# mLSTM of a hybrid block: the products of queries with states of both directions in three fp32r passes, the decay applied behind the product, and decay rows loaded one head ahead and masked in place

## The chip, the cores and the metric

One core of one Trainium2 chip runs the whole kernel as one program. The metric is device time in microseconds of one execution, the median of several runs. The engines named below are PE (TensorE matmul) with its weight loads (PEld), DVE (VectorE), ACT (ScalarE), POOL (GpSimd) and SP (SyncE, which only issues DMAs here).

## The reference, cut to what matters

The layer is one encoder block on 512 tokens of 1024 channels, all in float32: a combined projection, three token mixers (a bidirectional mLSTM with four heads of 128, neighbourhood attention, cross-attention into 256 memory tokens), a gated merge, an output projection, a gated FFN with a convolution, and a final norm. The change lies in the mLSTM. For one direction and one head the reference computes, chunk by chunk:

```python
inter_log = a + m_prev[..., None]
m_j = jnp.maximum(inter_log, jnp.max(D, axis=-1))
qk = jnp.einsum('bhcjd,bhcsd->bhcjs', q, k)
P = jnp.exp(D - m_j[..., None]) * qk
inter_w = jnp.exp(inter_log - m_j)
num = jnp.einsum('bhcjs,bhcsd->bhcjd', P, v) + inter_w[..., None] * jnp.einsum('bhcde,bhcje->bhcjd', C_prev, q)
den = jnp.sum(P, axis=-1) + inter_w * jnp.einsum('bhce,bhcje->bhcj', n_prev, q)
h = num / jnp.maximum(jnp.abs(den), jnp.exp(-m_j))[..., None]
```

The first term of `num` comes from keys inside the chunk; the second is the query times the state `C_prev` of all earlier chunks (for the backward direction, later ones), weighted by a decay per query. `den` is the same with the normaliser `n_prev`. The outputs of both directions are added and normalised per token and head.

## The kernel before, in words

**The big products.** A float32 product is made of three fp32r passes: each operand is split into a high part, rounded to fp32r, and the low rest; `mm3` (L212 to L215) issues high x high, high x low and low x high into one PSUM bank. The weights come in blocks of 128x1024 (512 KB) on SP's DMA queue into three raw buffers (L159). ACT makes the high part (L195), DVE the low part (L196), each in two halves per block, into four buffers for each part. All projections work on `mm` PSUM banks (four), the attention work on `at` banks (four). A helper `split_act` (L217 to L220) splits an activation in the same way.

**The order of the work.** The mixers are Python generators. `proj` emits one projection of 24 passes, and `step` (L1022) lets the oldest generator run for some of its steps in between: 1.25 steps after a projection of 512 columns in this stage (`RB`), 0.7 after a memory projection of 256 (`RM`). A scheduler then places the instructions on each engine, mostly in the order emitted, and later where an operand is not ready yet. PE, DVE and ACT each run their own list strictly in order. Small pieces of DVE and ACT work can be put off through the list `late`, which is emptied by `flush` in the second pass group of the next projection, or at the start of `states`.

**The mLSTM.** The 512 tokens are four blocks J of 128 and not the reference's chunks of 64: the same function in larger pieces. `ml_prep` (L549) makes the gates' cumulative sums; the rows cu - m, one number a token for each direction and head, go to DRAM as `rd`. `spread` (L621) makes the columns per block: `bi` (key side), `mh` (the maximum carried into the block), `wt` (weights of the keys in a state), `dec` (decay from state to state). Then, for each head h:

- `load_R` (L651): SP loads `rd[d, h]`, spread over all 128 partitions, into a tile R of 128x512, one for each direction; `mask` (L660) adds the triangle mask into a second tile `rm`. R and rm share four buffers, so one head fills them.
- `keys` (L666): four transposes of the keys, the split of the inner blocks' keys, and in `weigh` the values with weights, split as well.
- `states` (L696): the sums of each block into two `at` banks (blocks 1 and 2 with `mm3` on 258 columns for both directions, L709; blocks 0 and 3 as plain fp32 products of 129 columns, L707), then DVE and ACT chain them into three states a direction, `C[d][i]`, 128x129 each (128 values and the normaliser).
- `weights_J` (L726): the score product of keys and queries (L730, plain fp32, into columns 384 to 511 of a new `at` bank); ACT makes exp(rm + bi) for both directions (L734) and exp(R + mh) for each direction that has a state (L738); DVE multiplies the first with the scores (L739) and the second with the queries (L741).
- `values_J` (L744): on PE, for each direction, the weights times the values (L749) and, with `inter`, the weighted queries times the state (L751), both plain fp32 with 129 columns into columns 0 to 259 of the same bank. Then the denominators (ACT absolute value, DVE maximum and reciprocal), the sum of both directions in H (L757, L758) and the squares' sum (L760).
- `normalise` (L762): POOL raises to the power -0.5, DVE scales H (L769). `emit_y` (L771) transposes H and applies the output gate.

One step holds the weights of block J and the values of block J - 1, so the values of block 3 fall into the next head's first step, ahead of its states. `load_R` and `keys` of the next head are emitted in the step of block 3.

Of the kernel before, what the change touches and what calls it, by code (L numbers as in the profile page):

```python
# [17 lines left out]
P = 128  # L18
S = 512
# [91 lines left out]
def hybrid_block(ctx, tc, xg, xT, memT, wflat, vecs, gbias, nabias, outa, outb, outc):  # L111
# [437 lines left out]
    def ml_prep():  # L549
# [71 lines left out]
        def spread():  # L621
# [20 lines left out]
            ml.update(bi=bi, mh=mh, wt=wt, dec=dec)  # L642

# [3 lines left out]
    def ml_all():  # L647
# [3 lines left out]
        def load_R(h):  # L651
            R, rm = [], []
            for d in range(2):
                t = tp.tile([P, S], F32, tag="R", name=nm("R"), bufs=4)
                SY.dma_start(t, rd[d, h].partition_broadcast(P))
                R.append(t)
                rm.append(tp.tile([P, S], F32, tag="R", name=nm("R"), bufs=4))
            return R, rm

        def mask(R, rm):  # L660
            for d in range(2):
                with tc.issue_after(st["dve"]):
                    V.tensor_tensor(rm[d].rearrange("p (j c) -> p j c", j=4), R[d].rearrange("p (j c) -> p j c", j=4),
                                    msk[d].unsqueeze(1).to_broadcast([P, 4, P]), op=ALU.add)

        def keys(h):  # L666

# [5 lines left out]
            kh, kl = [u[:, o:o + 2 * P] for o in (1040, 1296)]  # L673
            ke = scr(2 * P)
            ew = tp.tile([P, S], F32, tag="H", name=nm("ew"), bufs=4)
            ew = [ew[:, o:o + 129] for o in (0, 132)]
# [3 lines left out]
            A.activation(ke.rearrange("p (j c) -> p j c", j=2), pt.rearrange("p (j c) -> p j c", j=4)[:, 0:4:3, :], AF.Copy)  # L680

# [11 lines left out]
            late.append(weigh)  # L693
            return (ke, kh, kl), (ew, wh, wl), C

        def states(h, k, w, C):  # L696

# [6 lines left out]
            for J in range(NT):  # L704
# [6 lines left out]
            for d in range(2):  # L711
                t = tp.tile([P, 2 * M], F32, tag="nab", name=nm("C"))
                C.append([t[:, o:o + 129] for o in (0, 132, 264)])
# [10 lines left out]
        def weights_J(h, J, R, rm):  # L724

            bi, mh = ml["bi"], ml["mh"]  # L726
# [3 lines left out]
            PE.matmul(kq, kT[:, hs], qT[:, hs], start=True, stop=True)  # L730
            E = tp.tile([P, 4, P], F32, tag="E", name=nm("E"))
            for d in range(2):
                with tc.issue_after(st["act"]):
                    A.activation(E[:, d, :], rm[d][:, js], AF.Exp, bias=bi[:, d, J, h:h + 1])  # L734
            ds = [d for d in range(2) if 0 <= J - 1 + 2 * d < NT]
            for d in ds:
                with tc.issue_after(st["act"]):
                    A.activation(E[:, 2 + d, :], R[d][:, js], AF.Exp, bias=mh[:, J - 1 + 2 * d, d, h:h + 1])  # L738
            V.tensor_tensor(E[:, 0:2, :], E[:, 0:2, :], kq.unsqueeze(1).to_broadcast([P, 2, P]), op=ALU.mult)  # L739
            a, b = 2 + ds[0], 3 + ds[-1]  # L740
            V.tensor_tensor(E[:, a:b, :], E[:, a:b, :], qT[:, hs].unsqueeze(1).to_broadcast([P, b - a, P]), op=ALU.mult)  # L741
            return E, ps

        def values_J(h, J, E, ps, C, H, ss):  # L744
            js = slice(J * P, (J + 1) * P)
            pv = ps[:, :260].rearrange("p (d c) -> p d c", d=2)
            for d in range(2):
                inter = 0 <= J - 1 + 2 * d < NT
                PE.matmul(pv[:, d, 0:129], E[:, d, :], va[:, J, h, 0:129], start=True, stop=not inter)  # L749
                if inter:  # L750
                    PE.matmul(pv[:, d, 0:129], E[:, 2 + d, :], C[d][J - 1 + d], start=False, stop=True)  # L751
            den = tiny(2)
            A.activation(den, pv[:, :, 128], AF.Abs)
            emv = em[:, J, :].rearrange("p (a b) -> p a b", b=4)
            V.tensor_tensor(den, den, emv[:, 0:9:8, h], op=ALU.max)
            V.reciprocal(den, den)
            A.activation(H[:, js], pv[:, 0, 0:128], AF.Copy, scale=den[:, 0:1])  # L757
            V.scalar_tensor_tensor(H[:, js], pv[:, 1, 0:128], den[:, 1:2], H[:, js], op0=ALU.mult, op1=ALU.add)  # L758
            sq = scr(128)
            A.activation(sq, H[:, js], AF.Square, accum_out=ss[:, J:J + 1])  # L760

        def normalise(H, ss):  # L762
# [3 lines left out]
            G.tensor_tensor(rs, v, nhalf[:, :4], op=ALU.pow)  # L766
            for J in range(NT):
                js = slice(J * P, (J + 1) * P)
                V.tensor_scalar(H[:, js], H[:, js], rs[:, J:J + 1], None, op0=ALU.mult)  # L769

# [13 lines left out]
        E = None  # L784
        R, rm = load_R(0)
        st_h = keys(0)
        yield
        for h in range(4):
            if prev:
                values_J(h - 1, 3, *E, C, *prev)  # L790
                normalise(*prev)
            states(h, *st_h)
            C = st_h[2]
            yield
            H = tp.tile([P, S], F32, tag="H", name=nm("H"), bufs=4)
            ss = tiny(4)
            mask(R, rm)
            E = weights_J(h, 0, R, rm)
            yield
            for J in range(1, NT):  # L800
                E2 = weights_J(h, J, R, rm)
# [9 lines left out]
        values_J(3, 3, *E, C, *prev)  # L811
        normalise(*prev)
        yield
        emit_y(3, prev[0])
# [651 lines left out]
```

## Time and profile before

| | |
|---|---|
| time, median of 3 runs | 876.23 us (875.88 to 876.34) |
| time of the profiled execution | 875.49 us |
| its span | 873.7 us |
| busy: PE, PEld | 868.3 us (99%), 736.4 us (84%) |
| busy: DVE, ACT, POOL | 587.7 us (67%), 466.2 us (53%), 125.0 us (14%) |
| mLSTM steps with states and values | about 120 to 231 us of the span |
| DMA | 99.81 MB, mean 114 GB/s |

A group's row gives line, engine, operation, out<-in by the program's names, shapes, count, then busy time, mean duration of one in ns, and the idle time of the engine just before, with what ended it. A timeline row gives start and duration in us; a row with x2 merges two instructions. A plain fp32 product appears as two instructions. Durations of matmuls overlap, so the time that one costs is the distance from its start to the next one's.

### The profile page before, as it was taken

How to read it: one execution, taken by the hardware profiler on the slowest of the kernel's cores; microseconds unless marked ns; L12 is line 12 of the kernel's file. 1: busy time of each engine (PE TensorE's matmuls, PEld its weight loads, DVE VectorE, ACT ScalarE, POOL GpSimd, SP SyncE). 2: the span in 40 equal slices, each digit the busy share in tenths (PEclk: the TensorE clock that was granted, in tenths of full speed). 3: DMA queues.
4: the chain of work that ended last, by engine and by line, in shares of the span. 5: the costliest groups of instructions: out<-in, count | busy, mean ns of one | idle time of the engine just before them, and what ended most of it. 6: DMA issues, size and time to landing. Idle time of an engine off the chain costs nothing.

```text
span 873.7 us, 12210 instructions
## 1 busy us (share of the span) xinstructions
PE 868.3 (99%) x4311; PEld 736.4 (84%) x4311; DVE 587.7 (67%) x1212; ACT 466.2 (53%) x983; POOL 125.0 (14%) x201
## 2 busy tenths in 40 slices
PE   9999999999999999999999999999999999999997
PEld 7898889888888888888888888888888888888887
DVE  7794687866577758897676658776633466666534
ACT  7563467755455658898544455444422344444532
POOL 0101100001163370600000002111100011111010
PEclk9999999999999999999999999999999999999999
DMA  8224623522252353533223432222233222222412
GB/s 281 99 79 154 203 98 120 182 84 98 97 138 78 112 157 109 157 122 120 97 97 109 145 108 97 97 97 96 76 100 110 101 97 98 98 96 89 128 47 97
DMA packets 39421, 99.81 MB, mean 114 GB/s; under 512 B 5688, under 2 KB 13880, under 8 KB 39360
## 3 DMA queue, kind: packets, MB, share of 16 engines
q1 hardware_dynamic: 31568, 92.32, 31.1%
q0 software_dynamic: 7360, 6.32, 3.3%
q8 instruction: 34, 0.56, 0.3%
q10 hardware_dynamic: 432, 0.39, 0.1%
q14 instruction: 27, 0.22, 0.1%
HBM read 94.80 MB, written 4.21 MB: 113 GB/s over the span
## 4 chain that ended last, share of the span: by engine, by line
PE 98%; DVE 1%; issue 0%; ACT 0%; POOL 0%; POOLq 0%
PE mm L213 29%; PE mm L214 29%; PE mm L215 29%; PE at L214 2%; PE at L215 2%; PE at L213 2%; PE at L896 1%; PE at L749 1%; PE at L877 1%; PE at L751 1%; PE at L858 0%; PE at L859 0%; PE at L730 0%; PE at L984 0%; PE at L243 0%
## 5 line engine op out<-in xcount | busy, mean ns | idle before, releaser
L213 PE MATMUL mm<-u,wh 128*128 128x512 f32 (+1 forms) x1072 | 415.2, 387 | 0.0
L215 PE MATMUL mm<-u,wl 128*128 128x512 f32 (+1 forms) x1072 | 411.9, 384 | 0.0
L214 PE MATMUL mm<-u,wh 128*128 128x512 f32 (+1 forms) x1072 | 411.6, 384 | 0.0
L195 ACT ACTIVATE wh<-wr 128x512 fp32r<-128x512 f32 (+2 forms) x298 | 184.0, 621 | 224.7 <-PE mm L214 175.2
L196 DVE TENSOR_TENSOR wl<-wr,wh 128x512 fp32r<-128x512 f32 (+3 forms) x300 | 204.1, 682 | 92.2 <-ACT wh L195 88.4
L215 PEld LDWEIGHTS mm<-u,wl 128*128 128x128 f32 x1072 | 201.4, 188 | 40.0 <-DVE wl L196 0.2
L213 PEld LDWEIGHTS mm<-u,wh 128*128 128x128 f32 x1072 | 201.6, 188 | 38.6 <-ACT wh L195 0.2
L214 PEld LDWEIGHTS mm<-u,wh 128*128 128x128 f32 x1072 | 201.6, 188 | 38.4
L1330 POOL TENSOR_TENSOR s<-s,rb 128x512 f32<-128x512 f32 x22 | 38.1, 1730 | 403.4 <-DVE s L1329 239.0
L542 POOL DMA_DIRECT2D u<-nav_d x128 | 62.2, 516 | 66.6 <-PE at L896 23.1
L219 ACT ACTIVATE u<-s 128x512 fp32r<-128x512 f32 x26 | 16.4, 631 | 57.7 <-DVE s L1333 56.3
L1333 DVE TENSOR_TENSOR s<-mm,s 128x512 f32<-128x512 f32 x22 | 15.2, 690 | 23.9 <-POOL s L1330 23.9
L462 ACT ACTIVATE s<-pad,vec 128x512 f32<-128x512 f32 x30 | 24.4, 814 | 9.8 <-DVE pad L460 9.8
L220 DVE SCALAR_TENSOR_TENSOR u<-s,u 128x512 fp32r<-128x512 f32 x26 | 19.1, 733 | 14.1 <-ACT u L219 14.0
L463 DVE SCALAR_TENSOR_TENSOR s<-pad,vec,s 128x512 f32<-128x512 f32 x30 | 22.5, 750 | 5.5 <-ACT s L462 5.5
L1329 DVE SCALAR_TENSOR_TENSOR s<-s,s 128x512 f32<-128x512 f32 x22 | 15.2, 692 | 13.4 <-ACT s L1328 13.3
L464 DVE SCALAR_TENSOR_TENSOR s<-pad,vec,s 128x512 f32<-128x512 f32 x30 | 22.5, 751 | 0.9
L1328 ACT ACTIVATE s<-s 128x512 f32<-128x512 f32 x22 | 13.9, 633 | 15.0 <-DVE s L1327 14.9
L460 DVE TENSOR_TENSOR pad<-mm,rb 128x512 f32<-128x512 f32 x22 | 15.1, 690 | 6.3 <-PE mm L215 6.2
L213 PE MATMUL mm<-wh,u 128*128 128x512 f32 x48 | 18.9, 394 | 0.0
L214 PE MATMUL mm<-wl,u 128*128 128x512 f32 x48 | 18.7, 390 | 0.0
L215 PE MATMUL mm<-wh,u 128*128 128x512 f32 x48 | 18.7, 390 | 0.0
(320 smaller groups left out, 1030.8 us busy)
## 6 DMA issues: line engine op xcount, KB each, us to landing
wr<-wflat SPq DMA_DIRECT2D x141, 512.0 KB, 3.3
nab<-nabias SPq DMA_DIRECT2D x16, 256.0 KB, 2.7
u<-nav_d POOLq DMA_DIRECT2D x128, 32.0 KB, 2.6
s<-xT SPq DMA_DIRECT2D x15, 256.0 KB, 3.7
wr<-wflat SPq DMA_DIRECT2D x14, 192.0 KB, 2.3
nav_d<-nv POOLq DMA_DIRECT2D x8, 256.0 KB, 2.8
R<-rd SPq DMA_DIRECT2D x8, 256.0 KB, 4.0
wr<-wflat SPq DMA_DIRECT2D x2, 544.0 KB, 3.3
```

The costliest lines, as they stand in the source:

```text
L195: A.activation(h[:, u:v], src, AF.Copy)
L196: V.tensor_tensor(l[:, u:v], src, h[:, u:v].bitcast(F32), op=ALU.subtract)
L213: PE.matmul(ps, lh, rh, start=start, stop=False)
L214: PE.matmul(ps, lh, rl, start=False, stop=False)
L215: st["mm"] = PE.matmul(ps, ll, rh, start=False, stop=stop).ins
L219: A.activation(h, src, AF.Copy, scale=scale)
L220: V.scalar_tensor_tensor(l, src, scale, h.bitcast(F32), op0=ALU.mult, op1=ALU.subtract)
L462: A.activation(t1, pad[:, 0:512], AF.Identity, scale=vcol(w, i), bias=vcol(b, i))
L463: V.scalar_tensor_tensor(t1, pad[:, 1:513], vcol(w, n + i), t1, op0=ALU.mult, op1=ALU.add)
L464: V.scalar_tensor_tensor(t1, pad[:, 2:514], vcol(w, 2 * n + i), t1, op0=ALU.mult, op1=ALU.add)
L542: G.dma_start(vw[r * 32:(r + 1) * 32, i * 256:(i + 1) * 256], nav_v[hf, r, CW[b]:CW[b] + 32, hp * 256:(hp + 1) * 256])
L1330: G.tensor_tensor(c, c, rb2, op=ALU.mult)
```

## The change: what it does

- Blocks 1 and 2, which have a state in both directions, no longer multiply the weighted queries with each state in plain fp32. The raw queries are split (high, low) in `keys`, and the two states that meet a block are laid side by side (258 columns) and split with `split_act` in `states`. In `values_J` of the block one `mm3` multiplies them, into columns 0 to 257 of the bank of the *next* block (`nxt`, whose scores are in columns 384 to 511). The decay per query, a new column `sc` made once for all heads in `spread`, multiplies the result behind the product: one DVE operation for the denominators, and two accumulations into H.
- Blocks 0 and 3 have a state in one direction only and keep the plain product; their weighted queries are made for both blocks at once in `edges`, two ACT exponentials and one DVE product a head.
- There is no `rm`: `edges` adds the mask in place, behind the exponentials that need the unmasked rows. The four buffers now hold two heads, and `load_R` of the next head is issued just behind `states` of this one, instead of in the step of block 3.
- `normalise` scales H on ACT instead of DVE, put off through `late`.

In the built program PE's list has 24 passes more and 16 plain products (32 instructions) fewer, and the same order outside the mLSTM steps.

```diff
+            for d in range(2):
+                sc = tot[:, 1:3, d, :]
+                V.tensor_tensor(sc, lfc[:, 1:3, 64 + 32 * d:68 + 32 * d], lfc[:, 1:3, 32 * d:32 * d + 4], op=ALU.subtract)
+                V.tensor_tensor(sc, sc, mh[:, 2 * d:2 * d + 2, d, :], op=ALU.add)
             A.activation(wt, wt, AF.Exp)
+            A.activation(tot[:, 1:3], tot[:, 1:3], AF.Exp)
...
-                rm.append(tp.tile([P, S], F32, tag="R", name=nm("R"), bufs=4))
-            return R, rm
-
-        def mask(R, rm):
+            return R
+
+        def edges(h, R, eq):
+
+            mh = ml["mh"]
+            for i in range(2):
+                J, d = 3 * i, 1 - i
+                A.activation(eq[:, i, :], R[d][:, J * P:(J + 1) * P], AF.Exp, bias=mh[:, J - 1 + 2 * d, d, h:h + 1])
+            qe = qT[:, h * S:(h + 1) * S].rearrange("p (j c) -> p j c", j=4)[:, 0:4:3, :]
+            V.tensor_tensor(eq, eq, qe, op=ALU.mult)
             for d in range(2):
-                with tc.issue_after(st["dve"]):
-                    V.tensor_tensor(rm[d].rearrange("p (j c) -> p j c", j=4), R[d].rearrange("p (j c) -> p j c", j=4),
-                                    msk[d].unsqueeze(1).to_broadcast([P, 4, P]), op=ALU.add)
+                r4 = R[d].rearrange("p (j c) -> p j c", j=4)
+                V.tensor_tensor(r4, r4, msk[d].unsqueeze(1).to_broadcast([P, 4, P]), op=ALU.add)
...
+            q = [u[:, o:o + 2 * P] for o in (1552, 1808)]
...
+            qs = qT[:, h * S + P:h * S + 3 * P]
+            A.activation(q[0], qs, AF.Copy)
+            V.tensor_tensor(q[1], qs, q[0].bitcast(F32), op=ALU.subtract)
...
+            if h > 0:
+                late.append(lambda: edges(h, R, eq))
...
+            tj = [tp.tile([P, 2 * M], F32, tag="nab", name=nm("C")) for _ in range(2)]
+            pair = lambda j, d: tj[j][:, 129 * d:129 * d + 129]
+            one = [t[:, 258:387] for t in tj]
+            C.extend([[pair(0, 0), pair(1, 0), one[0]], [one[1], pair(0, 1), pair(1, 1)]])
...
+            for j in range(2):
+                split_act(wh[j], wl[j], tj[j][:, :258])
...
-            ds = [d for d in range(2) if 0 <= J - 1 + 2 * d < NT]
-            for d in ds:
-                with tc.issue_after(st["act"]):
-                    A.activation(E[:, 2 + d, :], R[d][:, js], AF.Exp, bias=mh[:, J - 1 + 2 * d, d, h:h + 1])
...
-            a, b = 2 + ds[0], 3 + ds[-1]
-            V.tensor_tensor(E[:, a:b, :], E[:, a:b, :], qT[:, hs].unsqueeze(1).to_broadcast([P, b - a, P]), op=ALU.mult)
...
-                inter = 0 <= J - 1 + 2 * d < NT
+                inter = (J, d) in ((0, 1), (NT - 1, 0))
                 PE.matmul(pv[:, d, 0:129], E[:, d, :], va[:, J, h, 0:129], start=True, stop=not inter)
                 if inter:
-                    PE.matmul(pv[:, d, 0:129], E[:, 2 + d, :], C[d][J - 1 + d], start=False, stop=True)
+                    PE.matmul(pv[:, d, 0:129], eq[:, J // (NT - 1), :], C[d][J - 1 + d], start=False, stop=True)
             den = tiny(2)
-            A.activation(den, pv[:, :, 128], AF.Abs)
+            if nxt is not None:
+                pi = nxt[:, :258].rearrange("p (d c) -> p d c", d=2)
+                qs = slice((J - 1) * P, J * P)
+                mm3(nxt[:, :258], q[0][:, qs], q[1][:, qs], w[1][J - 1], w[2][J - 1], True, True)
+                sc = ml["sc"][:, J, :, h]
+                V.tensor_tensor(den, pi[:, :, 128], sc, op=ALU.mult)
+                V.tensor_tensor(den, den, pv[:, :, 128], op=ALU.add)
+                A.activation(den, den, AF.Abs)
+            else:
+                A.activation(den, pv[:, :, 128], AF.Abs)
...
             V.scalar_tensor_tensor(H[:, js], pv[:, 1, 0:128], den[:, 1:2], H[:, js], op0=ALU.mult, op1=ALU.add)
+            if nxt is not None:
+                V.tensor_tensor(den, den, sc, op=ALU.mult)
+                for d in range(2):
+                    V.scalar_tensor_tensor(H[:, js], pi[:, d, 0:128], den[:, d:d + 1], H[:, js], op0=ALU.mult, op1=ALU.add)
...
-            for J in range(NT):
-                js = slice(J * P, (J + 1) * P)
-                V.tensor_scalar(H[:, js], H[:, js], rs[:, J:J + 1], None, op0=ALU.mult)
+
+            def scale():
+                for J in range(NT):
+                    js = slice(J * P, (J + 1) * P)
+                    A.activation(H[:, js], H[:, js], AF.Copy, scale=rs[:, J:J + 1])
+
+            late.append(scale)
...
+            if h < 3:
+                R2 = load_R(h + 1)
             yield
...
                 if J == 3 and h < 3:
-                    R, rm = load_R(h + 1)
-                    st_h = keys(h + 1)
-                values_J(h, J - 1, *E, C, H, ss)
+                    st_h = keys(h + 1, R2)
+                values_J(h, J - 1, *E, *own, H, ss, E2[1] if J > 1 else None)
```

More of the change, by code (lines that the diff above doesn't have):

```diff
@@ L651, in load_R @@
         def load_R(h):
-            R, rm = [], []
+            R = []
             for d in range(2):
@@ L673, in keys @@
             kh, kl = [u[:, o:o + 2 * P] for o in (1040, 1296)]
-            ke = scr(2 * P)
-            ew = tp.tile([P, S], F32, tag="H", name=nm("ew"), bufs=4)
-            ew = [ew[:, o:o + 129] for o in (0, 132)]
+            ke = scr()
+            ee = tp.tile([P, S], F32, tag="H", name=nm("ee"), bufs=4)
+            eq = ee[:, :2 * P].rearrange("p (i c) -> p i c", i=2)
+            ew = [t[:, 2 * P:2 * P + 129] for t in (ke, ee)]
+            q = [u[:, o:o + 2 * P] for o in (1552, 1808)]
             C = []
@@ L693, in keys, with states @@
             late.append(weigh)
-            return (ke, kh, kl), (ew, wh, wl), C
-        def states(h, k, w, C):
+            if h > 0:
+                late.append(lambda: edges(h, R, eq))
+            return (ke, kh, kl), (ew, wh, wl), C, q, eq, R
+        def states(h, k, w, C, q, eq, R):
             flush()
@@ L784, in ml_all @@
         E = None
-        R, rm = load_R(0)
-        st_h = keys(0)
+        R = load_R(0)
+        st_h = keys(0, R)
         yield
@@ L789, in ml_all @@
             if prev:
-                values_J(h - 1, 3, *E, C, *prev)
+                values_J(h - 1, 3, *E, *own, *prev)
                 normalise(*prev)
             states(h, *st_h)
-            C = st_h[2]
+            own = st_h
+            R = own[-1]
+            if h < 3:
+                R2 = load_R(h + 1)
             yield
@@ L796, in ml_all @@
             ss = tiny(4)
-            mask(R, rm)
-            E = weights_J(h, 0, R, rm)
+            if h == 0:
+                edges(0, R, own[-2])
+            E = weights_J(h, 0, R)
             yield
             for J in range(1, NT):
-                E2 = weights_J(h, J, R, rm)
+                E2 = weights_J(h, J, R)
                 if J == 3 and h < 3:
-                    R, rm = load_R(h + 1)
-                    st_h = keys(h + 1)
-                values_J(h, J - 1, *E, C, H, ss)
+                    st_h = keys(h + 1, R2)
+                values_J(h, J - 1, *E, *own, H, ss, E2[1] if J > 1 else None)
                 E = E2
@@ L810, in ml_all @@
             prev = (H, ss)
-        values_J(3, 3, *E, C, *prev)
+        values_J(3, 3, *E, *own, *prev)
         normalise(*prev)
+        flush()
         yield
```

21 lines of the change are left out of this document (9 added, 12 removed).

## The prediction

> **What bounds the kernel now.** I read the page's part 1 first, then the chain that ended last (part 4), then the waits on PE, then the groups of the mLSTM stretch, and last the timeline there, matmul by matmul.
>
> ```profile
> span 873.7 us, 12210 instructions
> ...
> PE 868.3 (99%) x4311; PEld 736.4 (84%) x4311; DVE 587.7 (67%) x1212; ACT 466.2 (53%) x983; POOL 125.0 (14%) x201
> ...
> PE 98%; DVE 1%; issue 0%; ACT 0%; POOL 0%; POOLq 0%
> ```
>
> The first line is the span of the profiled execution; that execution took 875.49 us, so 1.8 us lie around the span, and it is 0.74 us under the median of 876.23. PE is busy for 99%, and the chain that ended last is PE for 98%. A busy PE can still hide waits, so the next view matters: the waits on PE, which has one row.
>
> ```profile
> PE at L243 <- PEq L1453: 0.8, 1, 0.8
> ```
>
> One wait of 0.8 us, at the very start. PE never waits for another engine after that. The consequence decides everything below: **time can leave only with PE work that goes, and time can come only with PE work added or with a wait that PE does not have today.** A shorter or longer DVE or ACT list is worth nothing by itself. By stage, the mLSTM steps run from about 115 to 235 us:
>
> ```profile
> 115.00:141.00 26.00, 26.00 (x133) 22.00 (x132) 21.21 (x63) 18.64 (x49) 1.87 (x3) 1.00 0.33 111
> 141.00:157.00 16.00, 16.00 (x138) 16.00 (x137) 12.29 (x38) 11.11 (x35) 1.01 (x1) 1.00 0.45 152
> 157.00:235.00 78.00, 78.00 (x418) 66.75 (x417) 53.26 (x144) 44.44 (x134) 4.63 (x6) 1.00 0.35 115
> ```
>
> The columns are the window, its length, then busy time of PE, PEld, DVE, ACT and POOL, granted clock (1.00, full), DMA share and GB/s. DVE fills 21.21 of 26, 12.29 of 16 and 53.26 of 78 us: loaded, with room.
>
> **Part by part: the state products on PE.** The prices are distances between starts in the timeline, not durations, because matmuls overlap.
>
> ```profile
> 139.57 0.39 PE L213 MATMUL mm<-u,wh 128*128 128x512 f32 x1
> ...
> 140.93 0.38 PE L730 MATMUL at<-u,u 128*128 128x128 f32 x2
> ...
> 141.15 0.39 PE L749 MATMUL at<-u,E 128*128 128x129 f32 x2
> 141.37 0.39 PE L751 MATMUL at<-C,E 128*128 128x129 f32 x2
> 141.60 0.39 PE L749 MATMUL at<-u,E 128*128 128x129 f32 x2
> ...
> 150.01 0.39 PE L707 MATMUL at<-ew,s 128*128 128x129 f32 x2
> 150.15 0.36 PE L213 MATMUL at<-u 128*128 128x258 f32 x1
> 150.35 0.28 PE L214 MATMUL at<-u 128*128 128x258 f32 x1
> 150.47 0.28 PE L215 MATMUL at<-u 128*128 128x258 f32 x1
> 150.59 0.28 PE L213 MATMUL at<-u 128*128 128x258 f32 x1
> 150.71 0.28 PE L214 MATMUL at<-u 128*128 128x258 f32 x1
> 150.83 0.28 PE L215 MATMUL at<-u 128*128 128x258 f32 x1
> 150.95 0.39 PE L707 MATMUL at<-ew,s 128*128 128x129 f32 x2
> ```
>
> A pass of 512 columns, the bulk of the kernel, takes 0.227 us (six of them from 139.57 to 140.93). A plain fp32 product of 129 columns stands as two instructions and takes (141.60 - 141.15)/2 = 0.225 us of PE. An fp32r pass of 258 columns takes 0.12 (150.35 to 150.83 in four steps). Changing from one kind to the other costs nothing extra: 150.01 to 150.95 is 0.94, and one pair plus six passes is 0.225 + 0.72 = 0.945.
>
> ```profile
> L751 PE MATMUL at<-C,E 128*128 128x129 f32 x48 | 9.3, 275 | 0.0
> ```
>
> These 48 instructions are 24 products (six a head: one for blocks 0 and 3, two for blocks 1 and 2). The change keeps the ones with a single state, 8 in all, and drops 16: 16 x 0.225 = 3.60 us leave. It adds, for blocks 1 and 2 of four heads, eight groups of three passes of 258 columns: 24 x 0.12 = 2.88 us come. The new passes have the shape of the ones priced, so the bound on each side is narrow: 0.119 to 0.125 a pass moves the sum by 0.1 us. **Net -0.72 us.** No other PE instruction is added or removed.
>
> The Trainium skill, in "FP8 and Floating Point Precision", section "TensorE Precision Notes", says that true fp32 makes four passes through the array; "VectorE: DVE Perf Modes", in its section on the TRN2 errata, gives a matmul max(60, 6 + columns) cycles at 2.4 GHz. By these an estimate for the old product is 4 x 56 = 225 ns, which the trace agrees with, and for a new pass 110 ns against the trace's 120; the sum would be -0.96 us instead of -0.72.
>
> **DVE and ACT, per head.** The rows are groups within 115 to 235 us.
>
> ```profile
> L758 DVE SCALAR_TENSOR_TENSOR H<-at,y,H 128x128 f32<-128x128 f32 x16 | 5.6, 348 | 2.4 <-ACT H L757 2.3
> ...
> L663 DVE TENSOR_TENSOR R<-R,msk 128x512 f32<-128x512 f32 x8 | 5.5, 690 | 6.4 <-DMA R<-rd 6.4
> ...
> L769 DVE TENSOR_SCALAR H<-H,y 128x128 f32<-128x128 f32 x14 | 3.5, 363 | 3.7 <-POOL y L766 3.7
> L741 DVE TENSOR_TENSOR E<-E,u 128x256 f32<-128x256 f32 x8 | 3.4, 420 | 0.2 <-ACT E L738 0.2
> ...
> L755 DVE TENSOR_TENSOR y<-y,em 128x2 f32<-128x2 f32 x16 | 2.5, 156 | 0.6 <-ACT y L753 0.6
> ...
> L741 DVE TENSOR_TENSOR E<-E,u 128x128 f32<-128x128 f32 x8 | 2.2, 281 | 0.1
> ```
>
> ```profile
> L738 ACT ACTIVATE E<-R,mt 128x128 f32<-128x128 f32 x24 | 8.8, 393 | 2.6 <-DMA R<-rd 2.6
> ...
> L219 ACT ACTIVATE X<-u 128x256 fp32r<-128x256 f32 x2 | 0.7, 404 | 0.0
> ```
>
> DVE loses two 420 and two 281 ns products (1.40) and four scalings of 363 (1.45). It gains one edge product (0.42), the low part of the queries and of two state pairs (3 x 0.42, taking 420 of the 128x256 form), and for blocks 1 and 2 three tiny operations of 156 and two accumulations of 348 (2 x 1.16). Net about +1.15 us. ACT loses six exponentials (2.36), gains two for the edges (0.79), three splits (3 x 0.40) and four scalings (4 x 0.35, the L757 form below): net +1.0 us. With the scalings, the wait for POOL (3.7 us in the L769 row) moves from DVE to ACT; behind it stand weight copies. The one-off decay terms for all heads are four tiny DVE operations and one ACT exponential, under 1 us. Over four heads that is +4.6 us on DVE, where the three windows have 120 - 86.8 = 33 us free. I cost it at nothing, under the cover of PE. None of these operations has been seen in its place; bounded from both sides, they cost the end between 0 and, if DVE became the bound there, those 4.6 us. I take 0, because the weight splits, which share DVE and ACT and feed PE, are themselves waiting for PE to free their buffers:
>
> ```profile
> L195 ACT ACTIVATE wh<-wr 128x512 fp32r<-128x512 f32 x43 | 26.7, 627 | 25.5 <-PE mm L214 20.7 <-ACT s L760 1.9 <-PE mm L215 1.5
> ```
>
> **Decay rows.** Of the 6.4 us for which DVE waited in the mask (L663 row), the rows' loads are the cause.
>
> ```profile
> R<-rd SPq DMA_DIRECT2D x8, 256.0 KB, 4.0
> ```
>
> Now both loads of a head are issued after the states of the head before, so the mask finds them landed. But PE did not wait for the mask, so nothing is won at the end. On SP the same eight 256 KB loads only stand earlier between the weight loads: in the new order three of them stand in a row in front of one weight load early on. If a weight load came one such landing late (4.0 us) PE would feel it only after the raw blocks and split halves held ahead run out, 24 passes of 0.227 us or 5.4 us for one block alone; bounds 0 to 4.0, taken 0. The masks in place add a wait behind the edge exponentials; behind it on DVE stand weight splits, which have the same cover.
>
> **The wait that is added.** The three passes write into the bank of the next block's score tile. That block's own values product writes there too, so PE now waits until DVE has read the state products out. Behind that values product on PE stands everything else. The chain of links in its old form, on the timeline:
>
> ```profile
> 187.21 0.17 ACT L753 ACTIVATE y<-at 128x2 f32<-128x2 f32 x1 [1.58 <-PE at L751]
> ...
> 187.41 0.16 DVE L755 TENSOR_TENSOR y<-y,em 128x2 f32<-128x2 f32 x1 [0.30 <-ACT y L753]
> ...
> 187.61 0.17 DVE L756 RECIPROCAL y<-y 128x2 f32<-128x2 f32 x1
> ...
> 187.86 0.35 ACT L757 ACTIVATE H<-at,y 128x128 f32<-128x128 f32 x1
> ...
> 188.25 0.35 DVE L758 SCALAR_TENSOR_TENSOR H<-at,y,H 128x128 f32<-128x128 f32 x1
> ```
>
> That is 1.39 us. The new chain puts two tiny operations in front (0.20 each with the hand-over) and two accumulations behind (0.35 + 0.03 each), 2.55 in all, and some 0.2 for the last pass to end: **2.75 us** undisturbed. Against it stands the PE work between the three passes and the values product in the new order, counted with 0.227 (512 columns), 0.12 and 0.225: 7.3 and 4.55 us in head 0, 6.0 and 5.0 in head 1, 5.4 and 5.2 in head 2, 5.0 and 2.95 in head 3. All eight cover 2.75; the last one barely.
>
> **Sum.** 875.49 - 3.60 + 2.88 = 874.8 for the profiled execution, and 876.23 - 0.72 = **875.5 us** for the median.
>
> **Rivals.**
>
> Small bank waits. If each chain takes 4.0 us, because a weight split of 0.69 or a wait for ACT falls into it, only the distance of 2.95 fails, by 1.05: 876.6. At 5.0 us the waits add up to 2.05 + 0.45 = 2.5. For it: DVE is 77% busy from 141 to 157 us, and queues run in order. Against it, from the list of who waits for the score product on DVE (L739):
>
> ```profile
>   PEld at L749: 0.4, 2
> ```
>
> Two weight loads already wait for DVE, 0.4 us in all, and PE loses nothing by it. Chance 0.20, with times from 875.9 to 877.9.
>
> The bank chain becomes the bound (the other side). If the chains take 5.5 us, the eight distances fail by 2.55 + 0.95 + 2 x 0.5 + 0.3 + 0.1 = 4.9 us: 880.4. It decides from a chain of 5.0 us on, where the waits exceed 0.72 + 1.75. That needs three weight splits in a chain, and the new order does put one to four of them into some; but those chains have long distances, and the chain with 2.95 has none. Chance 0.16. The Trainium skill, "PSUM — Partial Sum Buffer", section "PSUM bank collisions raise a hardware error", says to guard PSUM by bank and quadrant, not by address: by it the three passes must also wait until DVE has read the scores in the same bank. No run here shows it yet.
>
> More is won than counted. The 6.4 us of mask waits would have to be PE time in disguise; the waits on PE say no. If a third of them were, 873.4. Chance 0.04. That the rows are not really early is a rival too, but it changes nothing: 875.5 again.
>
> **How the numbers follow.** The likeliest is no new wait, chance 0.60, at 875.5 with 875.1 to 875.9 for run to run spread (three runs: 0.46 us). Within 0.2% (1.75 us, about what a measurement of this kernel can tell from no change) lie this and the small waits: 0.80. Slower 0.16, faster 0.04. The range reaches from 874.9 to 877.9, which takes in the first two cases.
>
> **What would show it.** Right: the span shorter by some 0.7 us, 16 instead of 48 instructions for the state products in plain fp32, 24 passes of 258 columns in the values step at 0.12 us each, no row of waits on PE but the first, the mask's waits for the loads gone, DVE some 5 us busier. Wrong: a wait on PE before the first values product of blocks 2 and 3, above all block 3 of the last head near 222 us, or a PE wait for a weight split near 145 to 157 us.

## The result, and the profile after

The changed kernel takes **877.68 us** (median of 20 runs, 877.00 to 878.12), the kernel before 875.91 us (20 runs, 875.64 to 876.49). The ratio is 1.0019, with a 95% interval from 1.0012 to 1.0026: 1.8 us slower where 0.7 us faster was forecast. It lies inside the forecast's range (874.9 to 877.9) and at the edge of what the forecast called no change, but the time went up where the forecast had it go down.

The page of the changed kernel, the same three lines as before:

```profile
span 875.8 us, 12232 instructions
...
PE 869.3 (99%) x4303; PEld 736.2 (84%) x4303; DVE 595.1 (68%) x1240; ACT 472.2 (54%) x996; POOL 125.0 (14%) x201
...
PE 93%; DVE 3%; ACT 2%; issue 1%; DMA 1%; POOL 0%; POOLq 0%; SPq 0%; ACTq 0%
```

PE is still busy for 99%, with eight instructions less. The third line tells most: the chain that ended last was PE for 98%, and now 93%, with 6% of it over DVE, ACT and DMA. A chain leaves an engine only where that engine waited. The waits on PE name the place:

```profile
PE at L213 <- DVE E L755: 0.8, 1, 0.8
PE at L243 <- PEq L1488: 0.8, 1, 0.8
```

The second row is the old one at the start. The first is new: a pass of `mm3` into an `at` bank waited for the score product on DVE (L755; L739 before). The three stretches of the prediction (window, length, busy time of PE, PEld, DVE, ACT, POOL):

```profile
115.00:141.00 26.00, 26.00 (x133) 22.00 (x132) 22.26 (x68) 18.87 (x49) 1.86 (x3) 1.00 0.36 123
141.00:157.00 16.00, 15.15 (x125) 14.73 (x124) 13.31 (x44) 10.96 (x35) 0.00 (x0) 1.00 0.53 165
157.00:235.00 78.00, 77.80 (x416) 65.63 (x415) 58.30 (x162) 47.23 (x140) 4.62 (x6) 1.00 0.31 105
```

PE lost 0.85 us in the middle stretch and 0.20 in the last. Here are PE and then DVE around the wait, in head 0 between the blocks 1 and 2 (start, length, engine, line):

```profile
141.40 0.38 PE L750 MATMUL at<-u,u 128*128 128x128 f32 x2
...
142.06 0.39 PE L750 MATMUL at<-u,u 128*128 128x128 f32 x2
142.29 0.49 PE L680 MATMUL at<-ident,u 128*128 128x128 f32 x3
143.63 0.39 PE L213 MATMUL at<-u 128*128 128x258 f32 x1 [0.85 <-DVE E L755]
```

```profile
140.41 0.69 DVE L674 TENSOR_TENSOR R<-R,msk 128x512 f32<-128x512 f32 x1
141.02 0.69 DVE L196 TENSOR_TENSOR wl<-wr,wh 128x512 fp32r<-128x512 f32 x1
141.62 0.42 DVE L671 TENSOR_TENSOR ee<-ee,u 128x256 f32<-128x256 f32 x1
141.96 0.69 DVE L674 TENSOR_TENSOR R<-R,msk 128x512 f32<-128x512 f32 x1
142.56 0.69 DVE L1081 TENSOR_TENSOR s<-mm,rb_x 128x512 f32<-128x512 f32 x1
143.16 0.41 DVE L755 TENSOR_TENSOR E<-E,at 128x256 f32<-128x256 f32 x1
```

DVE works without a gap. Ahead of the score product of block 2 stand two masks (L674) and an edge product (L671). They belong to **head 1**, whose first score product comes at 157.6 us: its rows are in early, the masks work in place and need no free buffer, so the scheduler put them here. From start to start they take 0.61, 0.34 and 0.60: 1.55 us. In the kernel before, DVE and PE stood like this at the same place:

```profile
141.13 0.69 DVE L1046 TENSOR_TENSOR s<-mm,rb_x 128x512 f32<-128x512 f32 x1 [0.74 <-PE mm L215]
141.74 0.41 DVE L739 TENSOR_TENSOR E<-E,at 128x256 f32<-128x256 f32 x1
```

```profile
142.27 0.60 PE L670 MATMUL at<-ident,u 128*128 128x128 f32 x4
142.70 0.39 PE L749 MATMUL at<-u,E 128*128 128x129 f32 x2
```

The product ended at 142.15 and PE took it up at 142.70: 0.55 us of cover, beside 0.74 us in which DVE idled. That is all the room there was.

The room shrank from PE's side too. Before, 1.77 us lay between the score product's start on PE (140.93) and the product that takes its result (142.70). After, it would be 1.11 us without the loss (141.40 to 142.51): the state products of block 1 no longer stand in between, and the passes come ahead of the fourth transpose. DVE's product ended 1.22 us behind that start before and 2.17 us after. So DVE came 0.95 us later and PE wanted the result 0.66 us sooner; less the 0.55 us of cover that makes 1.06 us, about what was lost there.

The row of 0.8 us is not the whole loss. For every kernel below I took, matmul by matmul, the distance from one end to the next, less the median distance of that shape, and added the places over 0.06 us between 120 and 240 us ("lost on PE" in the table). Before, there is none. After, there are five: 1.12 us at 143.63, 0.17 at 153.05, 0.20 at 173.79, 0.38 at 188.24 and 0.32 at 233.38, together **2.19 us**. With the forecast -0.72 of PE work this makes +1.47 of the measured +1.77. Taken directly, from the end of the 400th to the end of the 1000th pass of 512 columns (from about 121 to 303 us), PE needed 181.61 us before and 183.21 after: +1.60, which is 2.19 lost and 0.59 won. The first 10 us of any single profile lose another 0.5 to 1.5 us on PE, different from run to run for code that is not changed, so I compare medians and not spans.

### The profile page after: what moved, and what is told of

Read it like the earlier page. It is cut to its first block, busy times and chain, and to the rows that moved or that the text cites. A ratio compares the mean times of both kernels' runs of the same rounds, so it can differ in the third digit from the quotient of the medians.

```text
span 875.8 us, 12232 instructions
## 1 busy us (share of the span) xinstructions
PE 869.3 (99%) x4303; PEld 736.2 (84%) x4303; DVE 595.1 (68%) x1240; ACT 472.2 (54%) x996; POOL 125.0 (14%) x201
## 4 chain that ended last, share of the span: by engine, by line
PE 93%; DVE 3%; ACT 2%; issue 1%; DMA 1%; POOL 0%; POOLq 0%; SPq 0%; ACTq 0%
PE mm L213 27%; PE mm L214 27%; PE mm L215 27%; PE at L213 2%; PE at L214 2%; PE at L215 2%; PE at L931 1%; PE at L912 1%; PE at L763 1%; DMA R<-rd 1%; DVE wl L196 1%; PE at L893 0%; PE at L894 0%; PE at L1019 0%; PE at L243 0%
## 5 line engine op out<-in xcount | busy, mean ns | idle before, releaser
L196 DVE TENSOR_TENSOR wl<-wr,wh 128x512 fp32r<-128x512 f32 (+3 forms) x300 | 204.3, 682 | 89.0 <-ACT wh L195 86.6
L220 DVE SCALAR_TENSOR_TENSOR u<-s,u 128x512 fp32r<-128x512 f32 x26 | 19.1, 733 | 14.1 <-ACT u L219 14.0
L1375 DVE TENSOR_TENSOR u<-mm,u 128x512 f32<-128x512 f32 x13 | 9.0, 692 | 14.6 <-PE mm L215 14.6
```

Source lines behind the costliest of these rows:

```text
L196: V.tensor_tensor(l[:, u:v], src, h[:, u:v].bitcast(F32), op=ALU.subtract)
L220: V.scalar_tensor_tensor(l, src, scale, h.bitcast(F32), op0=ALU.mult, op1=ALU.subtract)
```

## The experiments

Theory B, held first: DVE's order is the cause; head 1's masks stand ahead of a score product that PE is about to need. Rivals: A, the shared bank alone makes PE wait (its columns 0 to 257 are written by the passes, 384 to 511 read by the score product); C, the added DVE and ACT work makes everything late wherever it stands; D, the early loads cost. Each was run in five rounds beside the kernel before on the same chip.

| kernel | us (11 runs) | before beside it | ratio, 95% interval | lost on PE |
|---|---|---|---|---|
| own_bank | 876.14 | 876.01 | 1.0000 (0.9991 to 1.0009) | 1.09 |
| masks_behind | 876.75 | 876.01 | 1.0009 (1.0000 to 1.0018) | 1.46 |
| passes_alone | 877.34 | 876.01 | 1.0015 (1.0006 to 1.0023) | 2.00 |
| late_rows | 877.80 | 876.01 | 1.0021 (1.0011 to 1.0030) | 2.35 |
| both | 875.56 | 875.96 | 0.9995 (0.9986 to 1.0004) | 0.42 |
| passes_first | 877.29 | 875.96 | 1.0013 (1.0004 to 1.0022) | 2.15 |
| first_behind | 875.46 | 875.96 | 0.9996 (0.9988 to 1.0005) | 0.46 |
| first_behind_2 | 875.59 | 876.00 | 0.9996 (0.9987 to 1.0005) | 0.47 |
| before_delay | 875.86 | 875.96 | 0.9999 (0.9990 to 1.0008) | 0.24 |
| rows_alone | 876.05 | 876.00 | 1.0002 (0.9993 to 1.0011) | 0.24 |
| own_first_behind | 875.12 | 876.00 | 0.9992 (0.9983 to 1.0002) | 0.13 |
| own_first_behind_2 | 875.08 | 876.11 | 0.9988 (0.9978 to 0.9997) | 0.13 |

**own_bank.**

```diff
+                nxt = mmps()
                 pi = nxt[:, :258].rearrange("p (d c) -> p d c", d=2)
```

> Edit: the three passes of blocks 1 and 2 write into a bank of their own from the projections' pool instead of the next block's score bank; everything else as in the changed kernel (877.7 us against 875.9 before; its largest PE wait is 1.1 us at 143.6 us, three passes behind the score product on DVE). Theory A (sharing the bank is the cause): the 1.1 us and the small waits go, 876.4 or less, 0.72 less PE work visible. Theory B (DVE reaches the score product late, because head 1's masks and edge product stand ahead of it in its list): the passes no longer wait, but the values product of block 2, which now follows some 0.6 us behind them, waits for the same score product; of the 1.1 us about 0.4 go, 0.7 stay, 877.2.

The wait moved as theory B had it, to the values product of block 2, behind the same score product. The waits on PE, and the row of the timeline:

```profile
PE at L763 <- DVE E L755: 0.7, 1, 0.7
```

```profile
144.09 0.71 PE L763 MATMUL at<-u,E 128*128 128x129 f32 x4 [0.70 <-DVE E L755]
```

0.96 us are still lost there. The time, 876.14, is A's number and not B's 877.2: the four smaller losses went too (0.13 left of 1.07), which neither text had counted. So the shared bank costs, but not at the place where theory A looked for most of it, and what own_bank shows at 144.09 is B's wait.

**masks_behind.** The edge product and the masks of heads 1 to 3 are held behind the last score product of the head before.

```diff
+            with tc.issue_after(st["kq"] if h > 0 else st["dve"]):
+                V.tensor_tensor(eq, eq, qe, op=ALU.mult)
...
-            V.tensor_tensor(E, E, kq.unsqueeze(1).to_broadcast([P, 2, P]), op=ALU.mult)
+            st["kq"] = V.tensor_tensor(E, E, kq.unsqueeze(1).to_broadcast([P, 2, P]), op=ALU.mult).ins
```

> Edit: the edge product and the two masks of heads 1 to 3 are held on DVE behind the last score product of the head before; banks, loads and arithmetic as in the changed kernel. Theory B (order on DVE): the score product of block 2 of head 0 runs some 1.7 us earlier (two masks of 0.60 and one edge product of 0.34, back to back, leave the stretch ahead of it), the 1.1 us of PE wait at 143.6 goes, 876.6 or less. Theory A (bank) expects a wait to stay wherever passes meet a score product, since the bank is shared as before: 877.5. Theory C (the added DVE and ACT work makes everything late, order or not): the wait moves to a later product, 877.5.

The banks are shared as in the changed kernel. DVE, then PE:

```profile
141.41 0.69 DVE L1082 TENSOR_TENSOR s<-mm,rb_x 128x512 f32<-128x512 f32 x1
142.02 0.41 DVE L756 TENSOR_TENSOR E<-E,at 128x256 f32<-128x256 f32 x1
```

```profile
142.10 0.49 PE L681 MATMUL at<-ident,u 128*128 128x128 f32 x3
142.48 0.39 PE L213 MATMUL at<-u 128*128 128x258 f32 x1
```

The score product starts 1.14 us earlier than after the change (DVE now idles 0.46 us for a weight's high part instead), and the passes follow the transposes after 0.38 us instead of 1.34. 0.96 of the 1.12 us are gone, by an edit that holds back three DVE instructions a head: B holds for this place, and A is no full cause. 876.75 lies just over B's 876.6: 0.9 us of time went, not the whole 1.8, and 1.46 us stay in six smaller losses, the largest 0.50 at 187.2, where a values product waits for its own score product.

**passes_alone.**

```diff
-                V.tensor_tensor(r4, r4, msk[d].unsqueeze(1).to_broadcast([P, 4, P]), op=ALU.add)
+                with tc.issue_after(st["dve"]):
+                    V.tensor_tensor(rm[d].rearrange("p (j c) -> p j c", j=4), r4, msk[d].unsqueeze(1).to_broadcast([P, 4, P]), op=ALU.add)
...
                 if J == 3 and h < 3:
+                    R2 = load_R(h + 1)
```

> Edit: the decay rows are treated as in the kernel before (loaded at block 3 of the head before, masked into a second pair of tiles, behind the weight products of DVE); the three fp32r passes, their shared bank, the edge products and the scaling on ACT stay. Theory B: the masks of head 1 stand behind the score products again, no wait of PE near 143.6, net of the PE sum (-0.72) and small waits 875.3 to 876.2. Theory A or C: the 1.1 us at 143.6 stays within 0.3, 877.3 or more.

A miss for B: 877.34 is the number of A or C, though the 1.12 us fell to 0.53, which neither had. The masks of head 1 do stand behind the score products here, yet PE still waits, because the edge product ahead of this one (0.33 us) is enough; without it, in masks_behind, 0.16 us are lost here:

```profile
141.94 0.42 DVE L673 TENSOR_TENSOR ee<-ee,u 128x256 f32<-128x256 f32 x1
142.27 0.69 DVE L1080 TENSOR_TENSOR s<-mm,rb_x 128x512 f32<-128x512 f32 x1
142.87 0.41 DVE L756 TENSOR_TENSOR E<-E,at 128x256 f32<-128x256 f32 x1
```

```profile
143.34 0.39 PE L213 MATMUL at<-u 128*128 128x258 f32 x1 [0.27 <-DVE E L756]
```

0.53 us are lost there, 0.25 at 129.45 (another product of DVE, behind a mask of head 0), 0.35 at a late score product (187.99), and the small bank losses stay. So the passes with their shared bank are slower without the masks too. The reason stands in rows of the changed kernel 30 us later, where no mask is near:

```profile
173.33 0.41 DVE L755 TENSOR_TENSOR E<-E,at 128x256 f32<-128x256 f32 x1
```

```profile
173.79 0.39 PE L213 MATMUL at<-u 128*128 128x258 f32 x1
```

The passes start 0.05 us after the product's end (173.33 + 0.41). It is so in all eight places, 0.05 to 0.25 us: the list of PE puts the passes just where they come free. The old values products had 2.7 to 6 us between score product and use in 13 of 16 blocks, and in seven of the eight whose score product the passes now wait for. **Sharing the bank turned a score product with microseconds of cover into one with next to none**, and any lateness of DVE beyond that goes straight to PE.

**late_rows.** Only the call of `load_R` for the next head goes back to block 3.

```diff
-            if h < 3:
-                R2 = load_R(h + 1)
...
                 if J == 3 and h < 3:
+                    R2 = load_R(h + 1)
```

> Edit: only the loads of the decay rows go back to block 3 of the head before; masks in place and all the rest as in the changed kernel. In DVE's list the masks of head 1 still stand ahead of the score product of block 2. Theory B: DVE now also waits there for the load to land (3 to 5 us after its issue), PE's wait at 143.6 grows to between 2 and 5 us: 878.5 to 881.5. Theory D (the early loads themselves cost, by making head 0's rows land 0.5 to 1 us later behind one another and so DVE and ACT late from 122 us on): the wait shrinks, 876.8 or less.

It tested neither theory, since the scheduler puts the loads where their buffers are free, not where the call stands. SP in the changed kernel and here:

```profile
119.59 1.33 SPq L660 DMA_DIRECT2D R<-rd  x3
```

```profile
119.20 1.33 SPq L660 DMA_DIRECT2D R<-rd  x3
```

The loads did not move, and 877.80 with 2.35 us lost is a second sample of the changed kernel. That the early loads cost (D) was left to rows_alone.

**both.** own_bank and masks_behind together.

> Edit: the two that each took away part are put together: the three passes write into a bank of their own, and the edge products and masks of heads 1 to 3 stand behind the last score product of the head before. Sum from the stalls seen so far: PE work -0.7 us, the wait of 0.96 us at 144.1 goes with the masks, the later bank waits of 0.2 to 0.5 us are gone with the bank, at most 0.2 us of waits left: 875.3 to 875.6, faster than the kernel before by 0.4 to 0.7 us. Rival (DVE and ACT work as such, wherever it stands): a wait of 0.5 us or more appears elsewhere and it is 876.0 or above.

As expected, 875.56. One loss is left, 0.42 us at 187.2, a values product behind its own score product:

```profile
185.03 0.43 DVE L220 SCALAR_TENSOR_TENSOR u<-C,u 128x258 fp32r<-128x258 f32 x1 [1.65 <-ACT u L219]
...
186.76 0.74 DVE L756 TENSOR_TENSOR E<-E,at 128x256 f32<-128x256 f32 x2
```

The rival's 0.5 us elsewhere and its 876.0 did not come, so the DVE and ACT work as such (C) is not the main cause. But this loss may be its share: the score product stands behind the new split of the states (L220), for which DVE idled 1.65 us until ACT was done. No run takes that split away alone.

**passes_first.** The passes go into the same shared bank ahead of the score product on PE, so they no longer wait for it.

```diff
             kq = ps[:, 384:512]
+            if J > 1:
+                qs = slice((J - 2) * P, (J - 1) * P)
+                mm3(ps[:, :258], q[0][:, qs], q[1][:, qs], w[1][J - 2], w[2][J - 2], True, True)
             PE.matmul(kq, kT[:, hs], qT[:, hs], start=True, stop=True)
...
-                mm3(nxt[:, :258], q[0][:, qs], q[1][:, qs], w[1][J - 1], w[2][J - 1], True, True)
```

> Edit: the three passes go into the same shared bank, but ahead of the next block's score product on PE instead of behind it; masks where the changed kernel has them. The passes then wait for nothing on DVE. If sharing the bank costs only by the wait for the score product to be read, the 1.1 us at 143.6 go, and the values product of block 2 stands some 26 passes later, so it does not take the wait over: 876.2 to 876.6. If DVE being late is what counts wherever it is met, a wait of 0.5 us or more stays at another instruction near 143 to 149 us: 877.0 or more.

The rival's case: 877.29. DVE is as late as before, and the loss turns up at the other end of the shared bank, where the next block's values product waits until DVE has read the state products out:

```profile
147.83 0.34 DVE L786 SCALAR_TENSOR_TENSOR H<-at,y,H 128x128 f32<-128x128 f32 x1
```

```profile
148.23 0.71 PE L766 MATMUL at<-u,E 128*128 128x129 f32 x4 [0.91 <-DVE H L786]
```

1.17 us are lost there, and 0.50 at 159.9, where PE waited for a weight's low part on DVE (L196).

**first_behind.** passes_first and masks_behind together, run twice.

> Edit: passes ahead of the score product in the shared bank, and masks of heads 1 to 3 behind the last score product of the head before. Against the kernel with masks behind alone (876.75) this takes away the waits of the passes (0.16, 0.19, 0.08 us) and starts each read-out earlier, so that the waits of values products for the bank (0.2 and 0.33 us) shrink: 875.7 to 876.2. If those waits come from chains that are queued on DVE and ACT, not from when they start, 876.5 or more.

> The kernel with passes ahead of the score product and masks behind, a second time, since its first ratio (0.9996, from 0.9988 to 1.0005) did not tell it from the kernel before. By its trace (PE work -0.7 us, waits +0.46 us within the mLSTM steps) 0.2 us are won for sure, by the first median 0.5 us: 875.4 to 875.8 beside a before of 876.0.

875.46 and 875.59, a little better than the first text had it; the waits on PE have only the row of the start in the first profile. Of the 2.15 us that passes_first lost, 1.69 are gone with the masks and the edge product held back; 0.46 stay.

**before_delay.** The kernel before, with work added.

```diff
+            for _ in range(5 if (h, J) == (0, 2) else 0):
+                V.tensor_scalar(E[:, 0:2, :], E[:, 0:2, :], 1.0, None, op0=ALU.mult)
```

> The kernel before with five multiplications by 1.0 (128x256, 0.34 us each back to back) on the decay factors of block 2 of head 0, ahead of their score product: 1.7 us more DVE work at that place and nothing else. In the trace of before the score product there ends at 142.15 and PE takes up the values product at 142.70, and DVE idles 0.75 us just ahead of it. Theory B (this place has no cover to speak of, whatever the change does): the product comes 1.0 to 1.3 us late and PE waits 0.4 to 0.9 us there: 876.4 to 876.9. If PE's cover is as wide as the busy shares say, no wait, 876.0.

I mispriced the addition. DVE, then PE:

```profile
139.45 0.28 DVE L740 TENSOR_SCALAR E<-E 128x256 f32<-128x256 f32 x1
139.63 0.42 DVE L743 TENSOR_TENSOR E<-E,u 128x256 f32<-128x256 f32 x1
...
142.64 0.41 DVE L741 TENSOR_TENSOR E<-E,at 128x256 f32<-128x256 f32 x1
```

```profile
142.53 0.60 PE L670 MATMUL at<-ident,u 128*128 128x128 f32 x4
143.11 0.49 PE L751 MATMUL at<-u,E 128*128 128x129 f32 x2
```

A multiplication holds DVE for some 0.2 us, not 0.34, so 1.0 us was added, and DVE no longer idles there. The product ends at 143.05, 1.86 us behind the start of its score product on PE (141.19) where it was 1.22 before, and PE loses 0.24 us. The cover of 0.55 us was used up by so little, which is B's point; in time, 875.86, it can't be seen.

**rows_alone.** Rows early, masks in place, scaling on ACT, but plain fp32 products with exponentials taken ahead of the mask, and no passes.

```diff
-                inter = (J, d) in ((0, 1), (NT - 1, 0))
+                inter = 0 <= J - 1 + 2 * d < NT
...
-            for j in range(2):
-                split_act(wh[j], wl[j], tj[j][:, :258])
...
-                values_J(h, J - 1, *E, *own, H, ss, E2[1] if J > 1 else None)
+                values_J(h, J - 1, *E, *own, H, ss)
```

> The other half by itself: decay rows loaded one head ahead and masked in place, all exponentials against the states taken ahead of the mask, scaling on ACT, but the products with the states in plain fp32 per block and direction as in the kernel before, no passes. In DVE's list the masks of head 1 come behind the score products of head 0. Theory B: no PE work changes and nothing stands ahead of the score products, so 875.8 to 876.3, no wait of PE over 0.3 us near 143. Rival (early rows and scaling on ACT cost by themselves): 876.6 or more.

876.05 beside 876.00: this half costs and wins nothing that the runs can tell, and D falls. In this order the masks of head 1 stand behind the score products of head 0. Those of head 0 (136.26) stand ahead of its first score product, whose cover falls from 2.80 us before to 0.06, and PE loses 0.24 us at 138.53: masks ahead of a plain product use up cover as well.

**own_first_behind.** All three mends, run twice; the edit is shown against first_behind.

```diff
+                pi = mmps()
-                mm3(ps[:, :258], q[0][:, qs], q[1][:, qs], w[1][J - 2], w[2][J - 2], True, True)
+                mm3(pi[:, :258], q[0][:, qs], q[1][:, qs], w[1][J - 2], w[2][J - 2], True, True)
```

> All three mends together: passes in a bank of their own and ahead of the next block's score product on PE, masks of heads 1 to 3 behind the last score product. The two double mends left 0.42 us (values product at 187.2 behind its score product) and 0.46 us (three waits of values products for the shared bank) of PE waits. If these are independent, 0.1 to 0.3 us stay: 875.1 to 875.4. Rival (the own bank brings the values product of block 2 forward to just behind its score product again): a wait of 0.3 us or more near 143 or 187 us, 875.5 to 876.0.

> The kernel with all three mends a second time, on the question whether it beats the kernel before by what the PE sum says. PE work -0.7 us and 0.13 us of waits left: 875.1 to 875.5 beside a before of 876.0, ratio 0.9990 to 0.9995. If the first median (875.12) was luck and the mends win nothing, 875.8 to 876.2.

875.12 and 875.08: **this version is 2.6 us faster than the changed kernel and about 0.1% faster than the kernel before**. The first interval against the kernel before still takes in 1, the second (0.9978 to 0.9997) does not. Its waits on PE have one row, the one at the start:

```profile
PE at L243 <- PEq L1491: 0.8, 1, 0.8
```

Over all runs one sum holds: the median less what was lost on PE is 875.0 to 875.5 us for each of the kernels with passes (877.68 - 2.19 = 875.5 for the changed one, 875.12 - 0.13 = 875.0 for the last) and 875.6 to 876.1 for those without.

## Why the prediction was wrong, point by point

**PE bounds, and time can come only with a wait.** Right, and it is what made the loss findable.

**Net -0.72 us of PE work.** Right. The groups show the counts (busy, mean ns of one; the 16 passes of each line are the eight of the states and eight new ones). The 600 passes of 512 columns above, with what was lost on PE taken off, take 181.6 to 181.7 us in the three kernels without passes and 180.7 to 181.1 in the others, so 0.5 to 0.9 us less:

```profile
L213 PE MATMUL at<-u 128*128 128x258 f32 x16 | 5.1, 322 | 0.8 <-DVE E L755 0.8
...
L765 PE MATMUL at<-C,ee 128*128 128x129 f32 x16 | 3.1, 275 | 0.0
```

The -0.9 and -1.0 us of own_first_behind, with 0.13 us of losses in them, are 0.3 to 0.4 us more than the sum. The intervals are wider than that, and I do not explain it.

**DVE and ACT per head, "I cost it at nothing, under the cover of PE".** This is the step that failed, together with the sentence on the masks, **"behind it on DVE stand weight splits, which have the same cover"**. What the runs showed in its place: the weight splits had cover in the changed kernel, since none of its five losses is at one (in passes_first 0.50 us were), but behind the masks stood a score product, which had 0.55 us. PE lost 1.12 us there, and holding the masks and the edge product back took 0.96 of them away. The cover was argued from busy shares and from one group of instructions, while the question was which instruction PE needs next in DVE's list, and how long before. The prediction quoted a hint and read it the wrong way round: two weight loads already waiting 0.4 us for the score product (at 186.23 and 214.19, where the values product followed 0.13 us behind it) meant that cover was gone there, not that waits cost nothing. The first of these places is where 0.38 us were lost after the change (188.24). The size was off as well: DVE has 7.4 us more (595.1 against 587.7) where 4.6 and under 1 were counted, ACT 6.0 where 4.0 were. The scalings, for one, were priced at 363 ns each, while their group row (14 of them in 3.5 us busy) gives 0.25 us each.

**Decay rows.** The loads' cost of 0 holds (rows_alone), and so does that the 6.4 us of mask waits were worth nothing:

```profile
L674 DVE TENSOR_TENSOR R<-R,msk 128x512 f32<-128x512 f32 x8 | 5.5, 689 | 0.4 <-ACT ee L669 0.4
```

The waits are gone from this row; 2.3 us of waiting for rows stand on ACT instead, in its edge exponentials (L669). But the waits on DVE had kept the masks out of the way: a mask that finds its rows at once may be placed anywhere, and it was.

**The wait that is added.** I priced the end of the bank's use, where the next values product waits for the read-out, and left its beginning, where the passes wait for the score product, to a sentence with "no run here shows it yet". In the changed kernel the passes start 0.05 to 0.25 us behind that product in all eight places. The Trainium skill, "PSUM — Partial Sum Buffer", section "PSUM bank collisions raise a hardware error", says to guard PSUM by bank and quadrant and not by address; the 0.85 us wait, for a read of other columns of the same bank, is what that guard looks like on PE's list. The wait should have been a term of the sum. The end was nearer: the read-out, put at 2.75 us undisturbed, took 3.2 to 7.6 us. In the last block of head 3, where the forecast saw a PE distance of 2.95 us, it is 3.2 us from the last pass to the end of the second accumulation:

```profile
230.04 0.28 PE L215 MATMUL at<-u 128*128 128x258 f32 x1
...
230.43 0.16 DVE L772 TENSOR_TENSOR y<-at,mt 128x2 f32<-128x2 f32 x1 [0.19 <-PE at L215]
...
232.50 0.74 DVE L785 SCALAR_TENSOR_TENSOR H<-at,y,H 128x128 f32<-128x128 f32 x2
...
233.38 0.46 PE L763 MATMUL at<-u,E 128*128 128x129 f32 x2
```

PE lost 0.32 us here, before a product that the forecast put near 222 us (before, it starts at 230.48). The first rival, small bank waits, thus came true at its place (with 0.17 at 153.05 it makes 0.5 us), but the larger part of the 2.19 us had no rival: 1.32 us at the bank's beginning (143.63 and 173.79) and 0.38 us at a late score product (188.24). That 877.68 still lies among this rival's times (875.9 to 877.9), and so inside the range, is luck: other waits filled it. The 0.2 us between the +1.60 above and the +1.77 of the medians are within the interval.

## What to carry to other kernels

Where one engine bounds at 99%, price each change on the other engines by the next thing the bound engine takes from their lists and by how long before it was ready, not by their busy shares. When a product moves into a bank that another product already uses, count a wait at both ends of the bank's use, the reads of other columns included. And work that is made ready earlier can be placed earlier, ahead of what is urgent: hold it back explicitly, or take its wait away last.

## What the runs showed of the hardware

A stop of PE cost 0.26 us more than its row: the wait of 0.85 us at 143.63 made the matmuls end 1.12 us late, and in own_bank 0.70 made 0.96, in passes_alone 0.27 made 0.53, in passes_first 0.91 made 1.17. On DVE a multiplication by a constant of 128x256 fp32 was followed by the next instruction after some 0.2 us, while a product of two tensors of that shape took 0.34 (139.63 to 139.97 in before_delay): the length column, 0.28 and 0.42, overstates both, as the next instruction starts before that length is over.
